# Twelve identity products on TensorE behind the first token block's transpositions, at the input of both feed-forward blocks

## The chip, the core and the metric

The kernel runs on one core of a Trainium2 chip. The metric is device microseconds from the first to the last instruction of a run. Three runs of the kernel before gave 829.69, 830.23 and 831.11 us; the median is 830.23 us. Engines are named as in the profile: PE (TensorE matmuls), PEld (TensorE weight loads), DVE (VectorE), ACT (ScalarE), POOL (GpSimd), SP (SyncE, which issues the weight transfers).

## What is computed

The reference runs two transformer layers one after the other on 256 tokens of width 1024, in float32. Each has a mixer (attention and a gated recurrent part; in the second layer a gated spatial part and a recurrent one) and a feed-forward block of hidden width 2816. Cut to what matters here:

```python
# layer 1
x  = x + gate_m * rms_norm(mix @ w..., g_post_mix)
h2 = rms_norm(x, g_pre_ffn) * (1 + scale_f) + shift_f         # input "f1"
ff = (silu(h2 @ w_ffn_gate) * (h2 @ w_ffn_up)) @ w_ffn_down
x  = x + gate_f * rms_norm(ff, g_post_ffn)
# layer 2
x  = layer_norm(ALPHA * x + gt1 * mix, ln1_g, ln1_b)
h  = x * (1.0 + sc2) + sh2                                    # input "f2"
f  = (silu(gu[..., :FFN_HIDDEN]) * gu[..., FFN_HIDDEN:]) @ w_ffn_out    # gu = h @ w_ffn_in
x  = layer_norm(ALPHA * x + gt2 * f, ln2_g, ln2_b)
```

## The kernel before, in words

**Tiles.** The 256 tokens are two blocks of 128, b = 0 and b = 1. Activations that enter a matrix product are held feature-major ("hT": 128 features on the partitions, 8 such groups, 256 tokens) and split into two reduced-precision parts, `hi` and `lo`; so is every weight slot of 128x1024 numbers (`whi`/`wlo`; `xhi`/`xlo` and `wx` are the same in other buffers). One product of float32 quality is three matmuls: hi by hi, hi by lo, lo by hi (`mm3`, L431). ACT makes `hi` by a cast, DVE makes `lo` by a subtraction.

**From tokens to hT.** After the last matmuls of a mixer or of a feed-forward block have gone to PSUM for token block b, a chain of small steps for that block does the residual and the norm (`chain_rms` L1064 for f1, `chain_ln` L1080 for m2 and f2) and calls `to_hT` (L1006): eight 128x128 transpositions on PE into two PSUM banks, a scale and shift into `hf` (four pieces on DVE, four on ACT), the cast of `hf` to `hT[0]` on ACT and the subtraction to `hT[1]` on DVE. Block 1 does the same some microseconds later. `ev` is the name of the input: "f1" and "f2" are the two feed-forward blocks, "m2" is the second mixer. Events `f1.0` and `f1.1` say that block 0's or block 1's share of hT is there. The stream of the big matmuls waits for `f1.0` and then uses block 0 alone for some weight slots (`tok_jobs` L891, with a lag of 3 slots for block 1).

**Order of the work.** From the first mixer's output product on, the order of the instructions on PE, DVE, ACT and POOL is worked out when the program is built, by a planner (`Plan`, L68 to 365) that reckons with a cost for every instruction; the program then holds each engine's instructions in just that order, and the trace has L376 for nearly all of them. SP's transfers are placed by the framework. Work comes from threads (Python generators) with ranks: the block chains have rank 0 (block 1 in the second layer 0.5), the stream of big matmuls rank 9, the split of a weight slot counts as rank 5 (`load`, L787 to 813), an adaptive-gate job on DVE (`part`) rank 8. When an engine comes free in the plan, `choose` (L152) takes the ready instruction of lowest rank, and of lowest sequence number among equals. An instruction is only known to the planner once its thread has been stepped to the place that issues it. A thread that stands at `yield GO` is stepped on when none of the PE instructions that it has issued is still waiting to be placed (`th.pe == 0`):

```python
    def start(self, th):                                                   # L98
        if th.go:
            return th.start if th.pe == 0 or th.rank == FILL and th.pe < AHEAD else math.inf
        ...
        th.pe += engine == "tensor"                                        # L252, when issued
        ...
        th.pe -= x.engine == "tensor"                                      # L338, when placed
```

In `to_hT` the only `yield GO` (L1017) stands between the transpositions and the pieces of `hf`. The planner counts a float32 matmul as 4 columns for one (L298, `w = 4 * n`), at 2400 columns a microsecond (L54), and doubles the variable part where it believes the clock of TensorE is low (L359).

**PSUM.** The tag `sm` has three banks of 128x512 (L2365). `to_hT` holds two of them for a block until its `hf` pieces have been read.

Of the kernel before, what the change touches and what calls it, by code (L numbers as in the profile page):

```python
# [18 lines left out]
P = 128  # L19
# [369 lines left out]
class Builder:  # L389
# [616 lines left out]
    def to_hT(self, xn, A, B, hT, b, ev):  # L1006

        nc = self.nc
        hf = self.scr.tile([P, D], F32, tag="s4", name="hf")
        pss = []  # L1010
        for q in range(2):
            x = xn(q)
            ps = self.pssm()
            for j in range(4):
                nc.tensor.transpose(ps[:, j * P:(j + 1) * P], x[:, j * P:(j + 1) * P], self.ident)
            pss.append(ps)
        yield GO  # L1017
        for q, ps in enumerate(pss):
            for j in range(4):
                k = q * 4 + j  # L1020
                o, i = hf[:, k * P:(k + 1) * P], ps[:, j * P:(j + 1) * P]
                if q == 0:
                    nc.vector.tensor_scalar(o, i, A[:, k:k + 1], B[:, k:k + 1], op0=ALU.mult, op1=ALU.add)
                else:
                    nc.scalar.activation(o, i, AF.Identity, scale=A[:, k:k + 1], bias=B[:, k:k + 1])
            h3 = hf[:, q * 512:(q + 1) * 512].rearrange("p (k t) -> p k t", k=4)
            hi = hT[0][:, q * 4:q * 4 + 4, b * P:(b + 1) * P]
            lo = hT[1][:, q * 4:q * 4 + 4, b * P:(b + 1) * P]
            nc.scalar.copy(hi, h3)
            nc.vector.tensor_tensor(lo, h3, hi.bitcast(F32), op=ALU.subtract)  # L1030
        self.plan.drop(hf, *pss)
        self.plan.set("%s.%d" % (ev, b))
# [1405 lines left out]
```

## Time and profile before

| | |
|---|---|
| median of the runs | 830.23 us (829.69 to 831.11) |
| the profiled execution's own time | 836.26 us |
| its span | 834.5 us |
| mean granted TensorE clock over the span | 0.975 of full speed |
| PE busy | 784.6 us, 94% of the span, 5912 instructions |
| DVE busy | 581.3 us, 70% |
| ACT busy | 379.8 us, 46% |
| POOL busy | 63.3 us, 8% |
| chain that ended last | PE 78%, DVE 8%, DMA 5%, ACT 3% |

[...] A bracket behind a timeline row gives the idle time of the engine before it and what ended it. The profiled execution is slower than the median run, so times of single instructions are taken from it and differences are added to the median.

### The profile page before, as it was taken

The numbers are of one execution on the slowest core, as the hardware profiler recorded it, in microseconds if no ns is written. First come the engines' busy times: TensorE is split into PE (matmuls) and PEld (weight loads), VectorE is DVE, ScalarE is ACT, GpSimd is POOL, SyncE is SP. The second block draws the span as 40 slices with busy tenths as digits, with TensorE's granted clock in tenths as the row PEclk, the third lists the DMA queues.
The fourth block names the chain that finished last, engine by engine and source line by source line (L and its number), as shares of the span: only waits on it lengthen the run. The fifth ranks groups of instructions, "written<-read, shape, count | busy, mean of one in ns | idle before, by whom it ended". The sixth has DMA issues, their size and how long they took to land.

```text
span 834.5 us, 14958 instructions
## 1 busy us (share of the span) xinstructions
PE 784.6 (94%) x5912; PEld 674.4 (81%) x5912; DVE 581.3 (70%) x1032; ACT 379.8 (46%) x599; POOL 63.3 (8%) x143
## 2 busy tenths in 40 slices
PE   5999899999979999999998999998897999999995
PEld 4778467899857999998875878876675899999884
DVE  3468866877678977876456467988549778667446
ACT  4346854454554444445425574443235444445330
POOL 3014010100020310000001011000101000000000
PEclk9999999999989999999999999999997999999999
DMA  9996489796759999997659618677434769966711
GB/s 273 318 280 179 159 290 281 208 247 179 245 160 307 272 307 262 305 303 243 186 168 261 165 51 199 155 232 219 153 103 156 219 191 293 251 200 202 254 51 51
DMA packets 205078, 178.94 MB, mean 214 GB/s; under 512 B 24052, under 2 KB 171712, under 8 KB 205008
## 3 DMA queue, kind: packets, MB, share of 16 engines
q1 hardware_dynamic: 201456, 168.37, 69.8%
q0 software_dynamic: 3552, 9.63, 3.5%
q8 instruction: 46, 0.75, 0.4%
q14 instruction: 24, 0.20, 0.1%
HBM read 175.06 MB, written 2.90 MB: 213 GB/s over the span
## 4 chain that ended last, share of the span: by engine, by line
PE 78%; DVE 8%; DMA 5%; ACT 3%; issue 3%; POOL 2%; SPq 1%; DVEq 0%; ACTq 0%; POOLq 0%
PE mm L376 51%; PE sm L376 6%; PE mm L434 4%; PE mm L435 4%; PE mm L436 4%; DMA raw<-in_w_in_dram 2%; PE ad L554 1%; DVE x L376 1%; POOL hr_r L376 1%; DMA base<-image 1%; PE ad L376 1%; DMA ada_raw<-in_w_ada_dram 1%; SPq L376 1%; DMA raw<-in_w_ffn_gate_dram 1%; DVE wlo L376 1%
## 5 line engine op out<-in xcount | busy, mean ns | idle before, releaser
L376 DVE TENSOR_TENSOR wlo<-raw,whi 128x1024 fp32r<-128x1024 f32 (+1 forms) x135 | 164.0, 1218 | 103.2 <-ACT whi L376 102.3
L376 ACT CAST whi<-raw 128x1024 fp32r<-128x1024 f32 (+1 forms) x135 | 140.9, 1045 | 190.3 <-PE mm L376 153.6
L376 PE MATMUL mm<-f_lo,whi 128*128 128x256 f32 x560 | 156.8, 280 | 0.0
L376 PE MATMUL mm<-f_hi,wlo 128*128 128x256 f32 x560 | 156.5, 279 | 0.0
L376 PE MATMUL mm<-f_hi,whi 128*128 128x256 f32 x560 | 156.1, 279 | 0.0
L376 PEld LDWEIGHTS mm<-f_lo,whi 128*128 128x128 f32 x560 | 105.9, 189 | 0.6 <-issue 0.5
L376 PEld LDWEIGHTS mm<-f_hi,whi 128*128 128x128 f32 x560 | 105.5, 188 | 0.3 <-issue 0.2
L376 PEld LDWEIGHTS mm<-f_hi,wlo 128*128 128x128 f32 x560 | 105.2, 188 | 0.7 <-issue 0.7
L427 DVE TENSOR_TENSOR wlo<-raw,whi 128x1024 fp32r<-128x1024 f32 x42 | 51.3, 1220 | 24.2 <-ACT whi L426 24.2
L426 ACT CAST whi<-raw 128x1024 fp32r<-128x1024 f32 x42 | 44.0, 1049 | 45.4 <-DMA raw<-in_w_in_dram 21.1
L434 PE MATMUL mm<-h_hi,whi 128*128 128x256 f32 (+1 forms) x184 | 52.8, 287 | 0.8 <-ACT qkv L1390 0.8
L436 PE MATMUL mm<-h_hi,wlo 128*128 128x256 f32 (+1 forms) x184 | 51.5, 280 | 0.0
L435 PE MATMUL mm<-h_lo,whi 128*128 128x256 f32 (+1 forms) x184 | 51.5, 280 | 0.0
L376 PE MATMUL mm<-m_hi,wlo 128*128 128x256 f32 (+1 forms) x152 | 43.2, 289 | 0.2
L376 PE MATMUL mm<-m_hi,whi 128*128 128x256 f32 (+1 forms) x152 | 42.9, 286 | 0.3 <-DVE kT L376 0.3
L376 PE MATMUL mm<-m_lo,whi 128*128 128x256 f32 (+1 forms) x152 | 42.6, 283 | 0.4 <-DVE vT L376 0.4
L434 PEld LDWEIGHTS mm<-h_hi,whi 128*128 128x128 f32 (+1 forms) x184 | 34.4, 187 | 3.1 <-ACT qkv L1390 1.7
L435 PEld LDWEIGHTS mm<-h_lo,whi 128*128 128x128 f32 (+1 forms) x184 | 34.1, 186 | 0.5 <-issue 0.5
L436 PEld LDWEIGHTS mm<-h_hi,wlo 128*128 128x128 f32 (+1 forms) x184 | 34.2, 186 | 0.0
L376 DVE SCALAR_TENSOR_TENSOR part<-ada_raw,cs,part 128x512 f32<-128x512 f32 x42 | 31.4, 748 | 0.6
L376 PE MATMUL mm<-wlo,hid_hi 128*128 128x512 f32 x80 | 31.3, 391 | 0.0
L376 PE MATMUL mm<-whi,hid_hi 128*128 128x512 f32 x80 | 31.2, 390 | 0.0
(548 smaller groups left out, 1784.0 us busy)
## 6 DMA issues: line engine op xcount, KB each, us to landing
ada_raw<-in_w_ada_dram SPq DMA_DIRECT2D x96, 512.0 KB, 6.0
raw<-in_w_in_dram SPq DMA_DIRECT2D x60, 512.0 KB, 5.4
raw<-in_w_ffn_in_dram SPq DMA_DIRECT2D x44, 512.0 KB, 5.0
raw<-in_w_ffn_gate_dram SPq DMA_DIRECT2D x22, 512.0 KB, 6.0
raw<-in_w_ffn_up_dram SPq DMA_DIRECT2D x22, 512.0 KB, 6.0
raw<-in_w_ffn_down_dram SPq DMA_DIRECT2D x22, 512.0 KB, 5.8
raw<-in_w_ffn_out_dram SPq DMA_DIRECT2D x22, 512.0 KB, 4.1
raw<-in_w_out_dram SPq DMA_DIRECT2D x16, 512.0 KB, 4.3
```

Source lines behind the costliest of these rows:

```text
L376: return lambda *args, **kw: self.plan.issue(self.name, op, args, kw, lambda: f(*args, **kw))
L426: self.nc.scalar.copy(hi, raw)
L427: self.nc.vector.tensor_tensor(lo, raw, hi.bitcast(F32), op=ALU.subtract)
L434: mm(out, lhsT=l[0], rhs=r[0], start=start, stop=False)
L435: mm(out, lhsT=l[0], rhs=r[1], start=False, stop=False)
L436: mm(out, lhsT=l[1], rhs=r[0], start=False, stop=stop)
L554: nc.tensor.matmul(ps[32 * g:32 * g + 32, :], lhsT=cv["rep"][:, 2 * (s - 1) + g, :], rhs=raws[s - 1 + g // 2][:, g % 2, :], start=s == 1, ...
```

## The change

Behind the transpositions of block 0 and ahead of the `yield GO`, `to_hT` takes a third `sm` bank and issues twelve float32 matmuls that multiply the identity with the first 128 columns of the last `x` tile. They overwrite the same 128 columns of the bank; nothing reads the bank and it is handed back at once. It is done for "f1" and "f2", not for "m2". No transfer, no DVE, ACT or POOL instruction is added or removed.

```diff
@@ def to_hT(self, xn, A, B, hT, b, ev):
                 nc.tensor.transpose(ps[:, j * P:(j + 1) * P], x[:, j * P:(j + 1) * P], self.ident)
             pss.append(ps)
+        if b == 0 and ev != "m2":
+
+            ps = self.pssm("warm")
+            for _ in range(12):
+                nc.tensor.matmul(ps[:, 0:P], lhsT=self.ident, rhs=x[:, 0:P], start=True, stop=True)
+            self.plan.drop(ps)
         yield GO
         for q, ps in enumerate(pss):
             for j in range(4):
```

## Rows read from the trace of the kernel before

**Rows 1.** The profile page, the granted TensorE clock in tenths, in 40 equal slices of the span (20.9 us each).
```profile
PEclk9999999999989999999999999999997999999999
```
**Rows 2.** Busy time by stretch: start and end in us, length, then PE, PEld, DVE, ACT and POOL busy (instructions), granted clock, DMA share, GB/s. The stretches around f1, the rest of layer 1's feed-forward block, the stretches around f2, and most of layer 2's feed-forward block.
```profile
236.57:239.98 3.41, 1.41 (x10) 0.88 (x9) 3.19 (x9) 3.41 (x8) 0.10 (x1) 1.00 0.57 163
239.98:246.81 6.83, 5.22 (x11) 3.23 (x12) 6.37 (x14) 2.85 (x8) 2.78 (x5) 0.50 0.65 192
...
251.20:436.00 184.80, 184.65 (x1249) 169.24 (x1250) 137.34 (x185) 81.09 (x101) 11.07 (x25) 1.00 0.88 261
...
632.50:642.75 10.25, 7.72 (x25) 5.69 (x26) 9.80 (x20) 5.55 (x11) 2.63 (x3) 0.50 0.54 148
643.00:800.00 157.00, 157.00 (x1118) 145.97 (x1117) 107.90 (x126) 71.84 (x88) 0.53 (x1) 1.00 0.77 227
```
**Rows 3.** Timeline of PE around f1: start us, us, engine, line, operation, out<-in, shapes, count. The first row is block 0's eight transpositions, the one at 246.60 block 1's.
```profile
236.89 1.09 PE L376 MATMUL sm<-ident,xn 128*128 128x128 f32 x8
241.38 0.79 PE L376 MATMUL mm<-whi,f_hi 128*128 128x512 f32 x1 [3.40 <-ACT f_hi L376]
...
242.66 0.80 PE L376 MATMUL mm<-whi,f_lo 128*128 128x512 f32 x1
...
245.38 0.63 PE L376 MATMUL mm<-whi,f_lo 128*128 128x512 f32 x1
245.81 0.63 PE L376 MATMUL mm<-whi,f_hi 128*128 128x512 f32 x1
246.60 1.18 PE L376 MATMUL sm<-ident,xn 128*128 128x128 f32 x8 [0.16 <-DVE xn L376]
...
248.98 0.39 PE L376 MATMUL mm<-wlo,f_hi 128*128 128x512 f32 x1
249.21 0.39 PE L376 MATMUL mm<-whi,f_lo 128*128 128x512 f32 x1
250.40 0.49 PE L376 MATMUL mm<-xhi,f_hi 128*128 128x512 f32 x1 [0.80 <-ACT xhi L376]
251.21 0.50 PE L376 MATMUL mm<-xlo,f_hi 128*128 128x512 f32 x1 [0.32 <-DVE xlo L376]
```
**Rows 4.** Timeline of PE around f2, same columns. The rows at 632.92 and 640.98 are the transpositions of block 0 and block 1.
```profile
632.92 1.94 PE L376 MATMUL sm<-ident,x 128*128 128x128 f32 x8 [2.77 <-DVE x L376]
636.97 0.79 PE L376 MATMUL mm<-whi,f_hi 128*128 128x512 f32 x1 [2.11 <-ACT f_hi L376]
...
638.09 0.79 PE L376 MATMUL mm<-whi,f_lo 128*128 128x512 f32 x1
...
640.98 1.92 PE L376 MATMUL sm<-ident,x 128*128 128x128 f32 x8
642.57 0.57 PE L376 MATMUL mm<-whi,f_lo 128*128 128x512 f32 x1
```
**Rows 5.** All instructions on the tile `vv` (layer 2's spatial gate), the PE ones: duration ns min/median/max, first and last start.
```profile
L376 PE MATMUL mm<-wsT,vv x16: 275/275/377, 572.8 to 589.0; 128*128 128x128 f32 x16
```
**Rows 6.** Timeline of PE, the second of the two places where those matmuls stand (at the full clock).
```profile
588.11 1.16 PE L376 MATMUL mm<-wsT,vv 128*128 128x128 f32 x8
```
**Rows 7.** Timeline of DVE around f1. `x` and the later `xn` belong to block 1, `hf` and `f_lo` to block 0, `wlo` to the stream's third weight slot.
```profile
239.26 0.40 DVE L376 TENSOR_SCALAR hf<-sm,afA,afsh 128x128 f32<-128x128 f32 x1
...
239.64 1.04 DVE L376 TENSOR_SCALAR hf<-sm,afA,afsh 128x128 f32<-128x128 f32 x3
240.60 1.40 DVE L376 SCALAR_TENSOR_TENSOR x<-res,rms_r,x 128x512 f32<-128x512 f32 x2
241.92 1.28 DVE L376 TENSOR_TENSOR f_lo<-hf,f_hi 128x512 fp32r<-128x512 f32 x2
243.12 1.22 DVE L376 TENSOR_TENSOR wlo<-raw,whi 128x1024 fp32r<-128x1024 f32 x1
...
246.05 0.89 DVE L376 TENSOR_SCALAR xn<-x,rms_r 128x512 f32<-128x512 f32 x2 [0.46 <-POOL rms_r L376]
```
**Rows 8.** Timeline of ACT around f1: the cast of that third slot, block 0's casts, then block 1's `hf` and the cast of the fourth slot.
```profile
237.90 1.04 ACT L376 CAST whi<-raw 128x1024 fp32r<-128x1024 f32 x1
...
240.71 1.14 ACT L376 CAST f_hi<-hf 128x512 fp32r<-128x512 f32 x2 [0.36 <-DVE hf L376]
...
247.81 1.51 ACT L376 ACTIVATE hf<-sm,afsh,afA 128x128 f32<-128x128 f32 x4 [4.58 <-PE sm L376]
...
249.71 2.20 ACT L376 CAST xhi<-raw 128x512 fp32r<-128x512 f32 x4
```
**Rows 9.** Timeline of DVE around f2. `hf` and `f_lo` at 634.87 and 637.36 are block 0's, `ln_ve` and `x` block 1's, `wlo` the second and third weight slot's.
```profile
634.87 1.36 DVE L376 TENSOR_SCALAR hf<-sm,f2A,f2B 128x128 f32<-128x128 f32 x4
...
636.27 1.17 DVE L376 TENSOR_TENSOR wlo<-raw,whi 128x1024 fp32r<-128x1024 f32 x1
637.36 1.28 DVE L376 TENSOR_TENSOR f_lo<-hf,f_hi 128x512 fp32r<-128x512 f32 x2
638.56 0.14 DVE L376 TENSOR_SCALAR ln_ve<-ln_mv 128x1 f32<-128x1 f32 x1
638.62 1.21 DVE L376 TENSOR_TENSOR wlo<-raw,whi 128x1024 fp32r<-128x1024 f32 x1
640.29 1.00 DVE L376 TENSOR_SCALAR x<-x,ln_mv,ln_r 128x512 f32<-128x512 f32 x2 [0.45 <-POOL ln_r L376]
```
**Rows 10.** Timeline of SP: the issue of the raw weights of the fourth slot.
```profile
225.47 0.37 SPq L376 DMA_DIRECT2D raw<-in_w_ffn_gate_dram  x1
```

## The prediction

> **What bounds the kernel now.** I read the page first: PE is busy 94% of the span, and its granted clock drops below full in few slices, among them the two that hold the inputs of the feed-forward blocks [rows 1]. Then the stretches. From 251.20 to 436.00 PE is busy 184.65 of 184.80 us, and from 643.00 to 800.00 all of 157.00 [rows 2]: behind either input PE never waits again for a long time, so what PE gains or loses at the input goes through to the end, microsecond for microsecond. The change stands in the two places where that is not so. At f1 PE ends block 0's transpositions at 237.98, sits idle 3.40 us for the cast f_hi, and runs at half clock from 239.98 to 246.81 [rows 2, 3]. At f2 it sits idle 2.77 us before the transpositions and 2.11 us behind them, and the half clock holds from 632.50 to 642.75 [rows 2, 4]. In such a stretch a 128x512 matmul starts every 0.43 us (245.38, 245.81), at full clock every 0.23 (248.98, 249.21) [rows 3]; eight transpositions take 1.94 us at f2 against 1.09 at f1 [rows 3, 4]. So something could be had here: 10 matmuls at f1 and 8 at f2, at 0.20 us each, and some 1.7 us of transpositions at f2.
>
> But where f1's stretch ends, PE isn't the bound: it has caught up and waits 0.80 us for the cast xhi and 0.32 for xlo [rows 3], which ACT does only behind block 1's hf (247.81), which waits for block 1's transpositions (246.60) and so for xn on DVE (246.05) [rows 7, 8]. At f2 PE goes on without a wait.
>
> **The price of the products.** No row shows a product with the identity as a plain float32 matmul. The nearest is the 128x128 float32 matmul of the spatial gate: the code has 8 of them (2 x 2 x 2) and the trace 16 records [rows 5], so two records each, and 8 records take 1.16 us with 0.275 for the last [rows 5, 6]: (1.16 - 0.275)/7 = 0.126 us per record, 0.25 per product. Twelve: 23 x 0.126 + 0.275 = 3.2 us at full clock; at half, with 0.43/0.23, up to 5.9. A lower end is the price of twelve transpositions, 1.09/8 x 12 = 1.6.
>
> At f1 they run at full clock from 237.85 to about 241.0 and lie in the gap of 3.40 us. Cost on PE: nothing. At f2 they start at 634.86 at half clock; if the clock comes back within a few microseconds of work they end near 638.4, if it does not near 640.8. Today's first matmul stands at 636.97 [rows 4], so without a later hf they would cost 1.4 to 3.8 us there.
>
> **The hidden part: the planner takes up hf later.** The products are issued ahead of the yield GO, and the chain is stepped on only when its last PE instruction has been placed (L98 to 100, L338). Until then the pieces of hf do not exist for the planner, and DVE and ACT are given whatever else is ready. Its own reckoning of a product is 512 columns at 2400 a microsecond, 0.21 us, or twice that where it believes the clock low (this sets an order and is no time): it holds hf back by 2.6 us at f1 and by more at f2. What is ready then is in the trace, now behind hf.
>
> f1, DVE: the third slot's wlo (1.22 us), today at 243.12, has its cast done at 238.94 [rows 7, 8]; it will go ahead of rms_m and hf. So rms_m, hf, x, f_hi and f_lo all come 1.2 us later: f_hi at 240.71 + 1.2, the first matmul at 242.6 for 241.38, the third (f_lo) at 243.9 for 242.66. At 243.12 there is 1.22 us less to do. No transfer is moved; the slot's raw buffer is given back sooner, and what POOL issues behind block 1's power comes 1.2 later, off the path (gate rows for the end of the block). Block 1's xn comes 5.45 us behind its x today (240.60, 246.05), with that wlo in between; if DVE alone sets that distance xn is where it was, if ACT's squares and POOL's power set it, 1.2 later. DVE waits 0.46 us for POOL just there [rows 7], so both have a hand; I take the middle, 0.7. PE gets through the 18 matmuls of the first three slots by about 250.0 even if the later half of today's slow stretch stays slow (to 246.81: 7 at 0.43, then 9 at 0.23 and 1.1 of transpositions), so xhi still ends last and f1 costs **+0.7**, with bounds -0.4 (xhi taken ahead of block 1's hf) and +2.
>
> f2, DVE: the second slot's wlo (1.17), block 1's ln_ve (0.14), the third slot's wlo (1.21) and block 1's x (1.00), today behind hf or f_lo [rows 9], go ahead of hf. The x needs POOL's power; it came 1.73 us behind ln_ve. From 634.87: wlo to 636.1, ln_ve, wlo to 637.4, x at about 637.8 to 638.75, hf 1.36 to 640.1, f_hi 0.6, first matmul at 640.8, that is 3.8 later. In return block 1's x is there before, so its transpositions, 1.92 us at half clock between the 8th and 9th matmul today [rows 4], run in the gap at full clock. But block 1's hf may come ahead of f_lo on DVE (up to three pieces, 1.04 us): f_lo at 641.1 to 641.8, the third matmul at 641.8, the ninth 6 x 0.23 later at 643.2. Today the ninth is at 642.57. f2 costs **+0.6**, with bounds -0.9 (f_lo ahead of those pieces, x at once) and +2.6 (half clock from 639 on).
>
> **Sum.** 0.7 + 0.6 = +1.3 us. The profiled execution took 836.26 us, 6.0 above the median, so it would read 837.6; on the median of 830.23 it is **831.5 us**. That is +0.16%, inside the 0.2% (1.7 us) below which a measurement can't tell a change of this kernel from none.
>
> One place decides it: may hf overtake the splits on DVE? The trace says no for ACT: the fourth slot's raw weights were issued at 225.47 and cast at 249.71, while ACT stood idle 4.58 us before 247.81 for something earlier in its order [rows 8, 10]. [...]
>
> **The rivals.** *The clock pays, hf is hardly late* (faster). If the planner finds little else to do in the hold, mm 1 at f1 stays near 241.4 and runs at full clock; the gain there ends at xhi, 0 to 1.1 us (the waits of 0.80 and 0.32). At f2 the first matmul is at 638.4 behind the products, 8 at 0.23 end at 640.2, and transpositions at full clock end at 641.9 instead of 642.57 or earlier if matmuls fill the wait: 0.7 to 1.7. Together about -2.3: **827.9 us**. For it: PE has nothing else to do in the gaps. Against it: rows 7 and 9 show wlo's ready to go. Chance 0.24.
>
> *The half clock comes all the same* (slower). Behind the products PE is idle again: at f1 from 241.0 to 242.6 and before f_lo, at f2 from about 639 to 640.8. Today idle PE of 3.40 and of 2.77 us was followed by half clock [rows 2 to 4]. It decides if the matmuls from 243.9 and 641.8 on run at 0.43 until all of f1's first 18 and f2's next 8 are through: f1, 16 at 0.43 and 1.94 of transpositions end at 252.7, where today's 19th stands at 250.4 and the 20th at 251.21, so that PE is some +1.7 behind; f2, +0.6 and 8 matmuls at 0.20 more, +2.2. Together +3.9: **834.1 us**. [...] Chance 0.22.
>
> *The order behind it falls out otherwise.* The planner sees f1 and f2 at other times, and may order layer 2's mixer, between the two, otherwise. A slow stretch of half the length of f1's costs 6.83/2 x (1 - 0.23/0.43) = 1.6 us; one more or less there, beside my sum, gives **833.1** or 829.9 us. Chance 0.14.
>
> *The products aren't done, since nothing reads them.* Then the hold-back stays and the clock falls as today: near the slower case's f1 and f2, with 834. Chance 0.02; the instructions stand in the program like any other.
>
> **How the numbers follow.** The forecast itself, between -0.4 and +2.5 us, has 0.38: 0.26 within 0.2%, 0.12 slower. The faster rival gives 0.22 faster and 0.02 within, the half clock 0.18 slower and 0.04 within, the order 0.03 faster, 0.06 within, 0.05 slower, the last 0.02 slower. That makes 0.25 faster by over 0.2%, 0.38 within, 0.37 slower. The range runs from the middle of the faster case to beyond the slower one: 827.8 to 835.0 us.
>
> **What would show it.** In the changed profile at f1: 24 records of products between 237.9 and 241; wlo ahead of hf on DVE, hf at 240.5, the first stream matmul near 242.6; full clock from 239.98 on. At f2: both wlo's and block 1's x ahead of block 0's hf, hf near 638.7, the first matmul near 640.8 behind block 1's transpositions. I am wrong if hf follows the transpositions at once as today, if the products reach beyond f_hi and PE waits for nothing there, or if the stretch from 251 to 436 shows new waits of PE.

## The result, and the profile after

The changed kernel took 843.12 us in the median (842.27 to 845.09, four runs), the kernel before, beside it, 830.67 (829.69 to 831.20). The ratio is 1.0129, with a 95% interval of 1.0088 to 1.0170: slower by 12.5 us between the medians, where the forecast was +1.3. (The ratio is not the quotient of the two medians, which is 1.0150; that lies in the interval too.) Medians and ratios here and below leave out executions more than 1.5% above the fastest of the same kernel (three of realigned's twelve, one of the kernel before). The profiled execution took 845.09 us (span 843.4), 2 us above its median; that of the kernel before was 6 us above its own.

At f1 the products, `wlo` and `hf` came as forecast; the clock and the end of the stage did not. PE's timeline, in answer to [rows 3]:

```profile
235.88 1.09 PE L376 MATMUL sm<-ident,xn 128*128 128x128 f32 x8
236.81 2.84 PE L376 MATMUL warm<-xn,ident 128*128 128x128 f32 x24
241.51 0.50 PE L376 MATMUL mm<-whi,f_hi 128*128 128x512 f32 x1 [1.85 <-ACT f_hi L376]
...
242.78 0.79 PE L376 MATMUL mm<-whi,f_lo 128*128 128x512 f32 x1 [0.54 <-DVE f_lo L376]
...
247.40 0.40 PE L376 MATMUL mm<-whi,f_hi 128*128 128x512 f32 x1
247.63 1.04 PE L376 MATMUL sm<-ident,xn 128*128 128x128 f32 x8
...
251.29 0.50 PE L376 MATMUL mm<-xhi,f_hi 128*128 128x512 f32 x1 [2.15 <-ACT xhi L376]
```

The 24 records lie in the gap. DVE and ACT, in answer to [rows 7, 8]:

```profile
238.25 1.22 DVE L376 TENSOR_TENSOR wlo<-raw,whi 128x1024 fp32r<-128x1024 f32 x1
...
239.45 1.36 DVE L376 TENSOR_SCALAR hf<-sm,afA,afsh 128x128 f32<-128x128 f32 x4
```
```profile
240.84 1.14 ACT L376 CAST f_hi<-hf 128x512 fp32r<-128x512 f32 x2 [1.50 <-DVE hf L376]
...
248.71 1.16 ACT L376 ACTIVATE hf<-sm,afsh,afA 128x128 f32<-128x128 f32 x3 [5.35 <-PE sm L376]
...
250.61 1.14 ACT L376 CAST xhi<-raw 128x512 fp32r<-128x512 f32 x2
```

The third slot's `wlo` is ahead of `hf`, and the first matmul stands 5.63 us behind the start of the transpositions instead of 4.49. But the 19th (`xhi`) stands 15.41 behind it, not 13.51: PE waits 2.15 us for that cast, which ACT has behind block 1's `hf`, which waits for block 1's transpositions, and these now stand behind 16 matmuls, where they stood behind 10. The stretches, in answer to [rows 2] (same columns), tell the rest:

```profile
238.97:242.70 3.73, 1.41 (x9) 0.79 (x7) 3.73 (x10) 2.20 (x7) 1.09 (x2) 1.00 0.77 226
242.70:246.10 3.40, 3.32 (x8) 2.65 (x9) 2.94 (x8) 0.66 (x2) 1.37 (x2) 0.50 0.68 224
252.90:256.30 3.40, 3.40 (x10) 2.63 (x9) 3.40 (x6) 1.36 (x2) 0.00 (x0) 0.50 0.84 249
256.30:436.00 179.70, 179.50 (x1230) 165.15 (x1229) 131.91 (x177) 78.35 (x95) 10.51 (x24) 1.00 0.86 259
455.00:461.20 6.20, 6.20 (x27) 3.32 (x26) 1.39 (x2) 1.04 (x1) 0.00 (x0) 0.51 0.93 258
638.60:642.00 3.40, 3.40 (x17) 3.40 (x17) 3.40 (x7) 1.51 (x4) 0.07 (x1) 0.50 0.17 20
646.00:800.00 154.00, 153.15 (x1088) 143.03 (x1089) 107.19 (x127) 72.02 (x90) 0.53 (x1) 1.00 0.77 226
```

Two stretches of half clock stand at f1, the second behind the wait of 2.15 us; the rest of the block shows no new wait. A third (455.00) is at the input of layer 2's mixer, which the change doesn't touch. In this pair of profiles PE loses more at that input than at any other place. Stretches of the kernel before and after, from block 0's transpositions at that input to the 49th matmul on it, and from there to block 0's transpositions at f2:

```profile
437.78:460.99 23.21, 20.16 (x135) 14.38 (x134) 15.08 (x29) 11.63 (x22) 3.83 (x6) 0.93 0.89 251
460.99:632.92 171.93, 158.29 (x1614) 130.18 (x1612) 118.73 (x270) 74.40 (x132) 13.82 (x16) 0.98 0.56 156
```
```profile
439.81:468.19 28.38, 24.81 (x167) 16.18 (x165) 15.24 (x30) 11.40 (x22) 3.84 (x6) 0.88 0.91 261
468.19:638.48 170.29, 157.74 (x1581) 130.49 (x1580) 118.81 (x269) 75.47 (x132) 13.78 (x16) 0.96 0.53 148
```

The first stretch is 5.17 us longer, with 32 PE instructions more in it: 24 `ad`, which make layer 2's adaptive rows, and 8 `adc`, which turn such rows into columns. The second has 33 fewer, but is only 1.64 us shorter. Of the 5.17 us, 4.65 are PE's busy time and 0.52 its idle time. The granted clock is lower in both stretches, 0.88 for 0.93 and 0.96 for 0.98: over the whole mixer that is about 20 us at half clock for 10 before. What stands where, in PE's timeline of before, then of after, and ACT's timeline of after:

```profile
445.63 0.40 PE L376 MATMUL mm<-wlo,m_hi 128*128 128x512 f32 x1
448.06 1.88 PE L376 MATMUL sm<-ident,x 128*128 128x128 f32 x8 [2.03 <-DVE x L376]
449.59 0.78 PE L376 MATMUL mm<-whi,m_lo 128*128 128x512 f32 x1
```
```profile
450.09 1.11 PE L376 MATMUL sm<-ident,x 128*128 128x128 f32 x8 [0.53 <-DVE x L376]
451.13 0.64 PE L376 MATMUL ad<-ada_raw,cs 128*32 128x256 f32 x8
453.79 1.44 PE L376 MATMUL adc<-sel,part 128*128 128x1 f32 x8 [2.02 <-ACT part L376]
455.08 0.77 PE L376 MATMUL mm<-whi,m_hi 128*128 128x512 f32 x1
```
```profile
451.24 1.16 ACT L376 ACTIVATE hf<-sm,m2B,m2A 128x128 f32<-128x128 f32 x3 [3.85 <-PE sm L376]
...
453.14 0.59 ACT L376 COPY part<-ad 128x512 f32<-128x512 f32 x1
```

Before, matmuls of the stream followed block 1's transpositions at once. After, `ad` and `adc` stand between, and `adc` waits 2.02 us for `part`, which ACT copies only at 453.14, behind block 1's `hf` (451.24). Most of that wait is no addition: before, PE stood 2.03 us ahead of block 1's transpositions, after, 0.53. At f2, in answer to [rows 4]:

```profile
638.48 1.83 PE L376 MATMUL sm<-ident,x 128*128 128x128 f32 x8 [2.76 <-DVE x L376]
640.10 3.77 PE L376 MATMUL warm<-x,ident 128*128 128x128 f32 x24
644.07 1.09 PE L376 MATMUL sm<-ident,x 128*128 128x128 f32 x8 [0.20 <-DVE x L376]
646.36 0.51 PE L376 MATMUL mm<-whi,f_hi 128*128 128x512 f32 x1 [1.21 <-ACT f_hi L376]
...
649.07 0.39 PE L376 MATMUL mm<-whi,f_lo 128*128 128x512 f32 x1
```

Block 1's transpositions come ahead of the first matmul, the clock is back (1.00 granted from 642.00 to 649.40), and the ninth matmul stands 10.59 us behind block 0's transpositions, where it stood 9.65. From the 19th matmul to the end of the span it then takes 192.02 us instead of 189.44, though PE is as busy there as before (the row from 646.00 on) and as fast by its granted clock.

### The profile page after: what moved, and what is told of

Same layout as the page of the kernel before. It is cut to its first block, busy times and chain, and to the rows that moved or that the text cites. A ratio compares the mean times of both kernels' runs of the same rounds, so it can differ in the third digit from the quotient of the medians.

```text
span 843.4 us, 15065 instructions
## 1 busy us (share of the span) xinstructions
PE 794.4 (94%) x5960; PEld 683.8 (81%) x5960; DVE 582.0 (69%) x1032; ACT 381.1 (45%) x599; POOL 63.2 (7%) x143
## 4 chain that ended last, share of the span: by engine, by line
PE 78%; DVE 11%; DMA 4%; issue 2%; ACT 2%; POOL 2%; SPq 1%; DVEq 0%; POOLq 0%; ACTq 0%
PE mm L376 52%; PE sm L376 5%; PE mm L434 4%; PE mm L435 4%; PE mm L436 4%; DMA ada_raw<-in_w_ada_dram 2%; DVE x L376 1%; PE ad L376 1%; PE ad L554 1%; DVE wlo L427 1%; DMA raw<-in_w_in_dram 1%; POOL hr_r L376 1%; DVE wlo L376 1%; DVE ln_st L376 1%; DMA XT<-image 1%
## 5 line engine op out<-in xcount | busy, mean ns | idle before, releaser
L435 PEld LDWEIGHTS mm<-h_lo,whi 128*128 128x128 f32 (+1 forms) x184 | 34.2, 186 | 0.5 <-issue 0.5
L436 PEld LDWEIGHTS mm<-h_hi,wlo 128*128 128x128 f32 (+1 forms) x184 | 34.2, 186 | 0.0
```

Of the source, the lines that this page charges most:

```text
L435: mm(out, lhsT=l[0], rhs=r[1], start=False, stop=False)
L436: mm(out, lhsT=l[1], rhs=r[0], start=False, stop=stop)
```

## The experiments

An edit is shown cut to the lines that matter; a remark behind # is not in the code. "The beat" is the planner's own: at each of its ticks the planner decides whether to reckon with the full or the half clock, so its phase, a constant, shifts later decisions.

Theory A: most of the loss lies in the order that the build-time planner makes, since the products shift its plan by 0.69 us. Theory B: the products' execution and the clock behind them cost it. Theory C: the hold-back of `hf` at the two inputs costs it. Ratios are to the kernel before on the same chip, with 95% intervals. Time differences inside a run are counted from the start of block 0's transpositions at the input in question.

**exec_only.** The products without the plan: behind the last transposition, unseen by the planner.

```
+            last = self.plan.thread.last
+            last.call = extra(last.call)   # the call, then twelve products issued past the planner
```

> The 24 products are executed behind the same last transpositions, but the planner doesn't know of them: the order of all other work is that of the kernel before, hf is not held back. Theory A (the loss is in the order that the planner makes of a plan shifted by 0.7 us; the work of the products costs little): 827 to 832 us, against 830.7 of the kernel before; at f1 the first stream matmul stays near 241.4 in the span, layer 2's second mixer as before. Theory B (the products' execution and the clock they leave behind cost it): 838 to 844 us, with the loss standing where the products stand or right behind.

830.15 us, ratio 0.9968 (0.9940 to 0.9996). The products themselves cost nothing; B has fallen. f1 ran at full clock throughout. First the stretch from 236 to 247 us of the kernel before, then the same of this one (granted clock 0.69 and 1.00), then this one's PE timeline:

```profile
236.00:247.00 11.00, 7.39 (x26) 4.78 (x25) 10.33 (x23) 6.47 (x14) 3.55 (x6) 0.69 0.60 178
```
```profile
236.00:247.00 11.00, 7.92 (x48) 6.12 (x46) 10.11 (x24) 6.09 (x16) 4.03 (x6) 1.00 0.63 198
```
```profile
235.52 2.84 PE L1024 MATMUL warm<-xn,ident 128*128 128x128 f32 x24
239.08 0.51 PE L376 MATMUL mm<-whi,f_hi 128*128 128x512 f32 x1 [0.72 <-ACT f_hi L376]
...
244.29 1.11 PE L376 MATMUL sm<-ident,xn 128*128 128x128 f32 x8 [1.83 <-DVE xn L376]
...
248.03 0.50 PE L376 MATMUL mm<-xhi,f_hi 128*128 128x512 f32 x1 [0.77 <-ACT xhi L376]
```

And still the 19th matmul is only 0.07 us earlier against the transpositions: what the clock gave, PE waited away, 1.83 us for `xn` and 0.77 for `xhi`. At f1 PE is not the bound.

**planned_only.** The plan without the products: the planner places them, but nothing is issued.

```
+        if self.mute:
+            call = lambda: None
```

> The planner reckons with the 24 products (the order and the hold-back of the changed kernel), but none is executed. Theory A: 839 to 844 us, as the changed kernel's 843.1; block 1's transpositions at the second mixer's input again 10.3 us behind block 0's and the 49th matmul there some 8 us later than before. Theory B: 829 to 833 us. If hf's delay alone mattered (theory C, the hold-back at the two inputs): 832 to 834 us.

845.15 us, ratio 1.0151 (1.0109 to 1.0194). The whole loss without one product (some 2 us more than the change, which the intervals don't tell apart). The 49th matmul of the mixer is 28.5 us behind block 0's transpositions, for 28.4 in the changed kernel.

**before_phase.** No product; another phase of the clock beat that the planner reckons with.

```
-        n = int((now + 0.8) / TICK)
+        n = int((now + 1.6) / TICK)
```

> The kernel before, without any product; only the phase of the clock beat in the planner's reckoning is 1.6 us instead of 0.8. The same instructions, in another order from the first feed-forward block's input on (724 of 3826 TensorE instructions at another place). Theory A: such a shift alone moves the time by several us, and by the order that comes out most of it at layer 2's mixer: 835 to 842 us. Theory B and C: no product, no hold: 829 to 833 us.

840.13 us, ratio 1.0087 (1.0051 to 1.0122). One constant of the planner, and no work added, moves the kernel by 7 to 8 us.

**after_phase.** The changed kernel with 2.4 in that line.

> The changed kernel, products executed and hold-back in force, with the planner's beat phase at 2.4 us instead of 0.8. Theory A: the order comes out otherwise and most of the loss goes: 828 to 834 us. Theory B and C: the products and the hold-back are as in the changed kernel, so 840 to 844 us.

841.83 us, ratio 1.0101 (1.0055 to 1.0146): a miss for A as I put it. The order did come out otherwise, but at the mixer's input the 49th matmul was again 28.4 us late and f1's 100th matmul 36.9. Another order isn't a better one.

**realigned.** The changed kernel with hold-back and products; the planner's beat is moved along by the 0.69 us, so that from the mixer's input to f2 the order on every engine is that of the kernel before.

```
-        n = int((now + 0.8) / TICK)
+        n = int((now + (0.8 if now < 37.0 else 0.11)) / TICK)
```

> The changed kernel, products executed and hold-back in force; in the planner's reckoning the clock beat is moved along by the 0.69 us by which the products shift the plan, so that layer 2's mixer is ordered as in the kernel before. Theory A (the mixer's order carries the loss): f1 +1.6 to +2 and f2 some +0.8 stay, the mixer costs nothing: 832 to 836 us; the 49th matmul of the second mixer no later against block 0's transpositions there than before (23.2 us), where the changed kernel has 28.4. Theory C (products and hold-back at the two inputs): 840 to 844 us.

839.90 us, ratio 1.0068 (1.0030 to 1.0106). The mixer's loss is gone: 23.33 us to the 49th matmul, and the granted clock is back.

```profile
439.72:463.05 23.33, 20.14 (x134) 14.14 (x133) 15.15 (x29) 11.62 (x22) 3.96 (x6) 0.93 0.86 250
463.05:632.24 169.19, 156.24 (x1613) 128.66 (x1612) 118.57 (x270) 74.37 (x132) 13.80 (x16) 0.99 0.56 158
```

But half of the loss remains, more than A allowed: C holds for a half.

**shifted.** The reverse: the kernel before, no product, no hold-back; the beat moved so that from the mixer's input to f2 the order is the changed kernel's on every engine.

```
-        n = int((now + 0.8) / TICK)
+        n = int((now + (0.8 if now < 37.0 else 1.49)) / TICK)
```

> The kernel before, without products or hold-back; behind the first feed-forward block's input the clock beat in the planner's reckoning is moved by the 0.69 us by which the products shift the plan. From the second mixer's input to the second feed-forward block's, the order is then the changed kernel's on every engine. Theory A: there the same loss as in the changed kernel, the 49th matmul 5.2 us later and 3 to 4 us left at the mixer's end, so 834 to 839 us beside 832 of the kernel before; f1 as before. Theory C: no difference, 830 to 834 us.

838.85 us, ratio 1.0062 (1.0033 to 1.0091), as A said:

```profile
438.99:467.03 28.04, 24.82 (x166) 16.32 (x165) 15.26 (x30) 11.40 (x22) 2.94 (x6) 0.88 0.91 265
467.03:636.82 169.79, 157.75 (x1581) 130.56 (x1580) 118.88 (x269) 75.34 (x132) 13.76 (x16) 0.96 0.53 148
```

The order of the mixer alone costs 0.62%, all but it 0.68%; together 1.30%, for 1.29% of the change. That they meet to 0.01% is luck, since each interval is 0.3 to 0.4% to either side. By the estimate under the table most of what this order costs is clock: shifted's runs were granted 0.9725 in the median and the kernel before 0.979 beside it; realigned's were granted 0.981, for 0.979.

**m2_warm.** The kernel before, with the planner told that the clock is full at the mixer's input alone.

```
-        return self.cold
+        return self.cold and not 219.6 < now < 224.9
```

> The kernel before, without products or hold-back; only at the second mixer's input the planner is told that the clock is full, which gives there the order of the changed kernel (four matmuls more of the adaptive rows ahead of block 1's transpositions, the four adc behind them). Theory A: the 49th matmul there comes about 5 us later than before, of which 3 to 6 are left at the mixer's end: 834 to 842 us. Theory C: 829 to 833 us.

840.35 us, ratio 1.0073 (1.0040 to 1.0107). The size is A's, the place only in part: the 49th matmul is 1.1 us late, the rest comes later in the mixer.

**f2_only.** The change at f2 alone.

```
-        if b == 0 and ev != "m2":
+        if b == 0 and ev == "f2":
```

> The change at the second feed-forward block's input alone, planned, held back and executed; up to there the order is that of the kernel before. Theory A: f2's term alone, +0.6 to +0.8 as in the changed kernel: 830 to 834 us, and the ninth stream matmul about 0.8 us later against block 0's transpositions than before (9.65). If f2 carries the loss: 838 or more.

838.32 us, ratio 1.0055 (1.0020 to 1.0090): a miss. The ninth matmul is 11.33 us behind the transpositions, for 9.65 before, and the block behind it is slower as well.

**exec_f2.** As exec_only, at f2 alone.

> As exec_only, but only f2's twelve products are executed; the order is that of the kernel before. In exec_only f1 ran wholly at full clock and still its 19th matmul came only 0.07 us earlier, while f2's came 0.9 earlier. If that is all that the products bring: the same time as exec_only, 827 to 832 us, with f2's ninth matmul 0.8 earlier against block 0's transpositions. If f1's clock does pay later: 830 to 833 us, with no gain left.

829.85 us, ratio 0.9963 (0.9928 to 0.9999), much the same as with f1's products: f1's bring nothing that shows.

**f2_nohold.** The change at f2, planned and executed, but the products are not counted in what holds `hf` back.

```
-        th.pe += engine == "tensor"
+        x.holds = engine == "tensor" and not self.nohold
+        th.pe += x.holds
```

> The change at the second feed-forward block's input alone, executed and planned, but the products don't count for the hold-back: hf's pieces are issued as before, and the order differs from the kernel before's in 6 places of TensorE and 5 of VectorE. f2_only, with the hold-back, took 0.55% more than the kernel before, exec_f2, unknown to the planner, 0.37% less. If the hold-back costs it at f2: as exec_f2, 828 to 832 us beside 832 of before, f2's 19th matmul 0.9 us earlier against block 0's transpositions, and the last 585 matmuls at 0.1133 us. If the place of the products in the plan costs it: as f2_only, 835 to 839.

830.22 us, ratio 0.9973 (0.9942 to 1.0004). Against f2_only only the hold-back has gone, and with it the loss. (With the hold-back goes the order that follows from it: the block is then ordered as in the kernel before, but for a few places.) DVE in f2_only, then here:

```profile
634.49 1.21 DVE L376 TENSOR_TENSOR wlo<-raw,whi 128x1024 fp32r<-128x1024 f32 x1
636.15 1.00 DVE L376 TENSOR_SCALAR x<-x,ln_mv,ln_r 128x512 f32<-128x512 f32 x2 [0.45 <-POOL ln_r L376]
637.07 2.64 DVE L376 TENSOR_SCALAR hf<-sm,f2A,f2B 128x128 f32<-128x128 f32 x8
```
```profile
629.03 1.21 DVE L378 TENSOR_TENSOR wlo<-raw,whi 128x1024 fp32r<-128x1024 f32 x1
630.15 1.36 DVE L378 TENSOR_SCALAR hf<-sm,f2A,f2B 128x128 f32<-128x128 f32 x4
```

`hf` starts 5.8 us behind block 0's transpositions (631.26) where it is held, and 1.95 (628.20) where it isn't.

**before_again.** The kernel before, for a second profile.

> The kernel before once more, for a second profile: how much of a stretch's length returns. Stretches with one order should agree within 0.3 us where the clock falls alike; the second projection of the second feed-forward block at 0.1133 us a matmul in its last 585, as in every profile without f2's hold-back. If the pace were chance, it could as well be 0.1178.

835.49 us. The pace came back at 0.1133, but the stretches agree less than expected: f1's block 0.4 us and the mixer 0.9 us longer, with the half clock at other places. So a single profile doesn't decide on 1 us in the mixer; the table below shows a spread of 6 us in one order.

**pace.** f2_only with a product behind every hundredth 128x256 matmul of f2 (nine ran, where I had reckoned with 25).

> The kernel with the change at f2 alone, and in that block's stream of 128x256 matmuls one product of the identity with itself behind every hundredth, unknown to the planner. In that kernel the last 838 matmuls run at 0.1178 us each from start to start. If an inserted matmul can turn the pace, stretches of 0.1133 appear that begin at an inserted product; if the pace belongs to the tiles or the stage, all stay at 0.1178. Of the whole time neither expects more than the 25 products themselves, 3 to 13 us, less up to 3.8 where the pace turns.

835.17 us in one run. Four stretches of the stream, behind the first, second, third and fourth product (a matmul lasts 0.28 us, so the counts take in two or three that reach over an edge):

```profile
666.40:677.20 10.80, 10.80 (x98) 10.80 (x97) 8.39 (x10) 4.05 (x5) 0.00 (x0) 1.00 0.82 250
677.80:682.50 4.70, 4.70 (x42) 4.70 (x42) 3.49 (x4) 1.63 (x3) 0.00 (x0) 1.00 0.88 274
690.80:698.90 8.10, 8.10 (x74) 8.10 (x73) 7.77 (x11) 4.29 (x5) 0.00 (x0) 1.00 1.03 279
703.10:714.50 11.40, 11.40 (x99) 11.40 (x99) 6.73 (x8) 5.24 (x6) 0.00 (x0) 1.00 0.86 230
```

All at full clock, without idle time, and from start to start in the timeline 0.1133, 0.1178, 0.1133, 0.1178 us: the pace turned from one product to the next.

**after_turn.** The changed kernel with one such product behind the fortieth matmul.

> The changed kernel with one product more of the identity with itself, unknown to the planner, behind the fortieth 128x256 matmul of the second feed-forward block. If the pace of the stream is a term of the loss: the matmuls behind it run at 0.1133 instead of 0.1178 us, some 800 times 4.4 ns less 0.2 for the product, so this block is 3.0 to 3.6 us shorter in the profile and the median 0.3 to 0.45% below the changed kernel's. If the pace only looks so in the records and something else sets the block's length: no change of the length, the median equal or 0.2 us more.

845.63 us, ratio 1.0166 (1.0137 to 1.0194): a miss. The product ran, but the 824 matmuls behind it stayed at 0.1178. In pace inserted products turned the pace; this one did not.

**after_again.** The changed kernel beside after_turn.

> The changed kernel once more, beside after_turn on one chip, and with a second profile: 842 to 845 us; f1's 19th matmul 1.9 us later than before against block 0's transpositions, the 49th of the mixer 5.2 later than before, the second feed-forward block's last 838 matmuls at 0.1178 us; whether the second stretch of half clock at f1 (252.9 to 256.3 in the first profile) comes back.

842.71 us, ratio 1.0138 (1.0114 to 1.0162). This execution had the half clock at f1 only from 251.0 on, behind the wait for `xhi`, and none at the mixer's input:

```profile
452.88 1.05 PE L376 MATMUL adc<-sel,part 128*128 128x1 f32 x8 [2.02 <-ACT part L376]
453.80 0.48 PE L376 MATMUL mm<-whi,m_hi 128*128 128x512 f32 x1
```

The same order with the same wait of 2.02 us, and the matmul behind it at full clock (0.48 us, for 0.77 at 455.08 in the first profile). f1's 19th matmul was 14.16 behind the transpositions, for 15.41; the mixer's 49th 26.87, 5.07 more than before_again's 21.80, which had full clock there too. So at the input the order is some 5 us later at either clock, though not by the same items: here 1.40 us of it is a wait for the transfer of `ada_raw`, in the first pair the half clock is longer by 3.4 us. To f2 little of it is left in this pair: the whole mixer takes 197.25 us for 196.08.

**All profiles by stage.** Lengths in us, over the profiles in which the stage has the same order and the same hold-back (their number in brackets); the four stages are the terms of the loss.

| stage | without | with | difference |
|---|---|---|---|
| f1, transpositions to the 100th matmul, `hf` held or not | 33.8 to 34.4, mean 34.2 (10) | 35.6 to 37.2, mean 36.6 (6) | +2.4 |
| second mixer, its transpositions to f2's, order of before or after | 190.3 to 196.1, mean 193.0 (8) | 197.3 to 198.7, mean 198.1 (5) | +5.1 |
| f2, transpositions to the 19th matmul, the change or neither products nor hold | 11.3 to 12.1, mean 11.8 (5) | 12.9 to 14.5, mean 13.6 (7) | +1.8 |
| f2, 19th matmul to the end, `hf` held or not (without pace and after_turn, which add products there) | 189.4 to 190.2, mean 189.5 (8) | 192.0 (6) | +2.5 |

The sum is 11.8 us; the medians differ by 12.5 and 11.0 in the two measurements. In the mixer's row PE's idle time is nearly alike, 15.6 us in the mean without and 16.1 with, but the time at half clock is 3.9 to 17.1 us without, mean 9.0, and 13.7 to 20.7 with, mean 19.2. Priced by f1's matmuls (0.43 us for 0.23, [rows 3]) the 10.2 us more cost up to 4.7 us, an estimate, of the 5.1. At f2 the products without hold-back give 11.0 to 11.2 (three profiles), 0.6 less than without them; hold-back without products gives 15.3.

## Why the prediction was wrong

**The products' price** was right: 24 records in 2.84 us at f1 (forecast 3.2), in the gap, at no cost. That f1's gain would end at `xhi` was right too: exec_only took all the half clock away there and won 0.07 us. (In the faster rival the -2.3 is no middle: its own terms give -0.7 to -2.8.)

**The hold-back at f1** went as described, `wlo` ahead of `hf`, first matmul 1.1 us later for a forecast of 1.2. No row of before showed whether `hf` may overtake the splits on DVE; here it did not: it started at 239.45 behind `wlo`, though the transpositions that it reads had ended at 236.97. The term was +0.7, by block 1's `xn`, and `xn` did come 0.72 us later (9.88 us behind block 0's transpositions for 9.16). What I left out is that six matmuls more now stand ahead of block 1's transpositions, so that these wait for PE and no longer for `xn`: half clock ahead of them, which cost nothing before, now counts. The 19th matmul came 0.7 later where the clock was full (after_again, 14.16 for before_again's 13.45) and 1.6 to 3.2 later in the five profiles with half clock there. To the 100th it is +2.4, since slow matmuls may also follow PE's wait of some 2.2 us for `xhi`. So my rival of the half clock, which had +1.7 for f1, held here in part; its +2.2 for f2 did not, in the changed profile. The same program met the half clock at f1 in two stretches in one execution (from 242.70 and from 252.90) and in one in another (from 251.0); what sets where it falls is not shown.

**The hold-back at f2** was right in its order on DVE (both `wlo`, then block 1's `x`, then `hf`) and in block 1's transpositions coming first. The term of +0.6 is +1.8 over all profiles, within its bounds of -0.9 to +2.6. f2_nohold shows that the hold and what it does to the order, not the products, makes it.

**The step that failed most is the order behind it.** The sum had nothing for it; as a rival with a chance of 0.14 it had 1.6 us either way, one slow stretch more or less. Measured it is +5.1 us. shifted shows +0.62% from it without a product, and realigned takes it away with the products in place. I wrote that the planner sees that stage at other times, and missed how far a plan 0.7 us later can go: 32 other instructions stand ahead of the stream at the input, and PE is 5 us late there. What is left of this at the mixer's end is mostly clock. So the price of a slow stretch was sound and their number was not: the time at half clock grew by 10.2 us, about three such stretches. Why this order meets more half clock is not shown.

**"What PE gains or loses at the input goes through to the end, microsecond for microsecond"** failed as well. Behind f2's 19th matmul, with no wait in the rows of either kernel, the block is 2.5 us longer wherever `hf` is held. f2_only and exec_f2, the same 66 us of stream:

```profile
694.00:760.00 66.00, 66.00 (x558) 65.52 (x557) 43.43 (x47) 30.53 (x36) 0.00 (x0) 1.00 0.77 213
```
```profile
694.00:760.00 66.00, 66.00 (x579) 65.52 (x578) 45.63 (x52) 31.85 (x37) 0.00 (x0) 1.00 0.81 227
```

PE is busy all of 66.00 us at full clock in both, and does 558 instructions in one and 579 in the other. A matmul's row lasts 0.28 us and the next starts 0.11 to 0.12 us behind it, so a busy share of 100% said nothing of the pace. The hold-back goes with the slow pace in every profile but pace's. But it also changes the order of the stream: without it a group of two matmuls (`adr`) stands behind 251 of the 128x256 matmuls (234 in shifted), and the pace turns there (at 695.44 in the kernel before); with it the group stands behind 174 (at 692.76 in the changed kernel) and nothing turns. No run separates hold-back and order, and after_turn, made to turn the pace, didn't; so the cause of these 2.5 us is open.

**The products' own gain** is small: three kernels with products and without hold-back took 0.27 to 0.37% less than the kernel before, with intervals that reach from 0.7% less to nothing; the stage at f2 shows 0.6 us of it, under 0.1%. What more there is in the medians I can't place: in exec_f2 nothing changes ahead of f2. Their runs were granted a clock of 0.9855 to 0.986 in the median, for 0.979 to 0.982 of the kernel before. So the best that the products gave is some 0.3 to 0.4%, and the intervals all but reach nothing.

## What to carry to other kernels

Where a planner orders the work, adding an instruction that "costs nothing" also moves every later decision: run the plan without the instruction and the instruction without the plan before believing either. A tuned order is one good draw among others; price a shift of it by what other orders of this kernel cost (here 5 to 8 us), not by one stall or one slow stretch. Before a longer stage is put down to its waits, compare its granted clock and PE's idle time: here the idle time was nearly the same. Let work that only keeps an engine busy stand where nothing is held back for it.

## What the runs showed of the hardware that was not expected

In these profiles a stream of 128x256 fp32r matmuls at full granted clock (1.00), without a recorded wait, ran at one of two steady paces, 0.1133 or 0.1178 us from start to start (4%), for hundreds of matmuls, and changed only where other matmuls stand between. In the kernel before nearly all of the last 596 of f2 run at the first, and the 251 ahead of them at the second; where `hf` is held and no product stands among them, all of the last 838 run at the second. In one kernel nine 128x128 products were inserted, and behind the first four the paces were 0.1133, 0.1178, 0.1133 and 0.1178 us; one in another kernel turned nothing; what decides is not known.
